# Row updates of five layer norms and the sums of a rotation, moved from GpSimd to VectorE in pieces

## The chip, the core and the metric

The kernel runs on one core of a Trainium2 chip. A core has a matrix engine (TensorE, PE in the profile), a vector engine (VectorE, DVE), a scalar engine (ScalarE, ACT), a general engine (GpSimd, POOL) and a queue engine that issues transfers (SyncE, SP). Each engine takes its instructions in order and waits for others on semaphores. The metric is the time of one execution on the device, in microseconds (us); of several runs the median is taken.

## The reference: what is computed

256 tokens of width 1024 pass through a first block of two layers in fp32. Each layer is a mixer, a cross attention to a memory of 256 tokens and a gated feed-forward net, with a layer norm of the scaled residual behind each:

```
for layer in range(DEPTH):                       # 2 layers
    mix = even_mixer(x, ...) or odd_mixer(x, ...)
    x  = layer_norm(DEEPNORM_ALPHA * x + mix, ln_g[layer, 0], ln_b[layer, 0])
    xa = memory_cross_attention(x, mem, ...)
    x  = layer_norm(DEEPNORM_ALPHA * x + xa, ln_g[layer, 1], ln_b[layer, 1])
    ff = swiglu(x, ffn_w_gu[layer], ffn_w_down[layer])
    x  = layer_norm(DEEPNORM_ALPHA * x + ff, ln_g[layer, 2], ln_b[layer, 2])

def layer_norm(x, g, b):
    ...
    return ((xf - mu) * lax.rsqrt(var + LN_EPS)).astype(x.dtype) * g + b

def rope(t):                                     # the odd mixer's queries and keys
    ...
    return jnp.concatenate([t1 * cos - t2 * sin, t1 * sin + t2 * cos], axis=-1).astype(t.dtype)
```

The even mixer joins a gated linear recurrence (mLSTM) and a neighbourhood attention, whose queries are scaled by 1/8 before a bias is added to the scores. The odd mixer is a differential attention with rotated queries and keys. A second block of two layers follows (convolutions, attention, and 16 experts); the change does not touch it.

## The kernel before

**Dense products.** Weights come as units of 128x2048 (`ring`, 1 MB) on SP's queue. `split` (L199) cuts each half of a unit exactly into two parts, `wh` (a copy on ScalarE, L126) and `wl` (the rest, a subtraction on VectorE, L123); the activations are split likewise into `xh` and `xl`. Three products (wh·xh, wh·xl, wl·xh) give fp32. A unit of 512 columns over 1024 rows is two `ring` loads, so four splits, of 12 products of 128x512 each. `wh` and `wl` have two buffers each, so a split's `wh` waits until TensorE is through with the split before the last. Work at the side is woven in: units of the modulation of the second block (`ada`: products with `scT`, then `adae`, then sums `mods`), and stretches of work (`fill`) such as the memory's keys and values (`mem_kv`) or the context's projection.

**Layer norms.** `resid` makes z = ALPHA·x + mix with its statistics; `ln_finish` (L288) takes them together, normalises z (first half on VectorE, L117, second on ScalarE, L132), transposes it by TensorE into X (`to_T`: `tov` copies from psum, then `xh` on ScalarE and `xl` on VectorE, with gain and bias by column), runs a `fill`, and then makes the new x itself, token-major: x = z·g, x = x + b, four GpSimd instructions of 128x1024, with g and b as rows broadcast over partitions (`lnbc`, two loads per norm). The products that follow read X; x is next read by the residual of the following norm. Six norms stand in the block; the last one makes x otherwise, so five have these updates. They follow the even mixer, cross attention, feed-forward, odd mixer and cross attention; below they are the first to fifth norm.

**Rotation.** `rope` (L708) makes for each of two token blocks four products with cos and sin out of psum (into `rtmp` and `tk`, VectorE) and two sums (`tk<-tk,rtmp`, GpSimd). `odd_mixer` does so for the first four of six units (0 and 1 are queries, 2 and 3 keys); the results are transposed by TensorE and copied into `qk` and `cpad`.

**Neighbourhood attention.** The bias `nab` is multiplied by 8 and the mask added, both on GpSimd; the softmax scales scores plus bias by 0.125.

**Order.** The instructions of each engine stand in an order that a scheduler sets at build time by priorities and dependences: `fill`, the modulation and the main line are ranked by it, and a tile whose memory another tile held waits for the last use of that one. z and the attention's queries `qk` share one slot; the odd mixer's slots lie where the slots of the feed-forward, with its norm's `lnbc`, were.

Of the kernel before, what the change touches and what calls it, by code (L numbers as in the profile page):

```python
# [46 lines left out]
class Net:  # L47
    def __init__(self, tc, a, out):
        self.tc, self.nc, self.a, self.out = tc, tc.nc, a, out
        self.S, self.bank = "M", "acc"  # L50
        self.wide, self.turn = False, 0
        self.tags, self.side, self.bg, self.ticks, self.every = {}, None, None, 0, 2
        self.later = []
        self.conv, self.rate, self.due = iter(()), (0, 0), 0.0

# [1 line left out]
    def ps(self):  # L57
        """psum for attention and transposes; work that fills gaps keeps off the bank ring it would wait for"""
# [5 lines left out]
    def open(self, side, **tags):  # L64
        """a pool of slots, by tag; closed in the reverse order on each side"""
# [12 lines left out]
    def t(self, shape, name, dt=F32, kind=None):  # L78
        """a slot of the smallest class that holds the tile"""
# [6 lines left out]
    def big(self, shape, name, dt=F32):  # L86
        """a slot that outlives the phase, where there are such"""
# [34 lines left out]
    def tt(self, out, in0, in1, op, eng=None):  # L122
        (eng or self.nc.vector).tensor_tensor(out=out, in0=in0, in1=in1, op=op)  # L123
# [16 lines left out]
    def rsqrt(self, v, n, g=None):  # L140
        """Newton's steps from the exponent's half; the steps' scales multiply to one"""
# [22 lines left out]
    def fill(self, n, bank="acc"):  # L164
        """n steps of the work at the side"""
# [10 lines left out]
    def after(self, f):  # L176
        """a part that waits for others: with the next step, where the work fills gaps"""
# [5 lines left out]
    def tick(self, n=1):  # L183
        """a modulation unit after every other unit of weights"""
# [15 lines left out]
    def split(self, src, eng=None, to=None):  # L200
        h, l = to or (self.tags[k][0].tile([128, 1024], F32R, name=k, bufs=self.tags[k][1]) for k in ("wh", "wl"))
        self.cp(h, src)
        self.tt(l, src, h.bitcast(F32), OP.subtract, eng=eng)
# [9 lines left out]
    def dense_unit(self, X, w, u, n=512, accs=None, nk=8):  # L213
        """[256, nk*128] @ [nk*128, n]; units of 2048 columns per partition."""
# [19 lines left out]
    def hl(self, X, c0, n, src, scale=1.0):  # L234
        """exact split of src (chunks c0..c0+n) into X's two parts"""
# [7 lines left out]
    def to_T(self, X, src, nch, g=None, b=None, c0=0, val=None):  # L243
        """src(t, c) token-major [128, 128] blocks -> chunks c0.. of X (or of val), times g plus b"""
# [17 lines left out]
    def acc_to_T(self, acc, t, dst, n=4, scale=1.0):  # L262
        """token-major psum [128, n*128] -> dst [128, n, 128]"""
# [24 lines left out]
    def ln_finish(self, z, st, x, i, fill, last=False):  # L288
# [25 lines left out]
        self.fill(fill)  # L314
        for t in range(2):
            self.tt(x[:, t], z[:, t], gb[0], OP.mult, eng=self.nc.gpsimd)
            self.tt(x[:, t], x[:, t], gb[1], OP.add, eng=self.nc.gpsimd)
# [11 lines left out]
    def softmax_T(self, scores, nh, nk, scale, bias=None, sinks=None):  # L329
        """scores(j, t, psum) fills [128 queries, nk*128] for head j of nh, block t of queries;  # L330
        -> the heads' [128 keys, nk, 256 queries] and their psum banks, free again.
        Two heads lie on different partitions, so that their products run side by side."""
# [60 lines left out]
    def even_mixer(self):  # L393
# [21 lines left out]
        # gates: rows i fwd, i bwd, f fwd, f bwd of 4 heads  # L415
# [7 lines left out]
        # log sigmoid of the forget gates  # L423
# [10 lines left out]
        for u, dst in ((2, bqT), (3, bkT)):  # L434
            accs = self.dense_unit(X, w, u)
            for t in range(2):
                self.acc_to_T(accs[t], t, dst[:, :, t * 128:(t + 1) * 128])
# [14 lines left out]
        # conv over tokens and silu; chunks 0..3 queries, 4..7 keys  # L452
# [25 lines left out]
    def mlstm(self, qk, vx, G, lf):  # L478
# [16 lines left out]
        # scores, transposed: [key, query] within a chunk  # L495
# [10 lines left out]
        for step in range(2):  # L506
            for d in range(2):
                t = step if d == 0 else 1 - step
                # transposed layout [s, l]: forward keeps s <= l
# [9 lines left out]
                if step == 0:  # L519
# [7 lines left out]
                    # state after this chunk  # L527
# [56 lines left out]
                for h in range(4):  # L584
                    o = hs[:, t, h * 128:(h + 1) * 128]
                    # block t: forward comes first for t == 0, backward for t == 1
# [7 lines left out]
    def neighbourhood(self, bqT, bkT, bv, Y):  # L594
        nc = self.nc
        rows = [slice(0, 64), slice(64, 128)]
        for hp in range(4):
            bias = []
            for hh in range(2):
# [3 lines left out]
                nc.gpsimd.tensor_scalar(b2, b2, 8.0, 0.0, op0=OP.mult, op1=OP.add)  # L603
# [6 lines left out]
            pts, P = self.softmax_T(scores, 2, 2, 0.125, bias=lambda j: bias[j])  # L610
# [1006 lines left out]
```

## Time and profile before

| | |
|---|---|
| three runs | 2421.43, 2418.28, 2417.38 us; median 2418.28 |
| profiled execution, span | 2420.6 us |
| TensorE busy | 2097.0 us (87%) |
| VectorE busy | 1186.0 us (49%) |
| ScalarE busy | 710.9 us (29%) |
| GpSimd busy | 105.0 us (4%), 64 instructions |

The profile gives, for one execution, each engine's busy time, groups of instructions by line and operation, time lines, and for idle time before an instruction what released it. [...]

### The profile page before, as it was taken

How to read it: one execution, taken by the hardware profiler on the slowest of the kernel's cores; microseconds unless marked ns; L12 is line 12 of the kernel's file. 1: busy time of each engine (PE TensorE's matmuls, PEld its weight loads, DVE VectorE, ACT ScalarE, POOL GpSimd, SP SyncE). 2: the span in 40 equal slices, each digit the busy share in tenths (PEclk: the TensorE clock that was granted, in tenths of full speed). 3: DMA queues.
4: the chain of work that ended last, by engine and by line, in shares of the span. 5: the costliest groups of instructions: out<-in, count | busy, mean ns of one | idle time of the engine just before them, and what ended most of it. 6: DMA issues, size and time to landing. Idle time of an engine off the chain costs nothing.

```text
span 2420.6 us, 26953 instructions
## 1 busy us (share of the span) xinstructions
PE 2097.0 (87%) x10408; PEld 1247.9 (52%) x10408; DVE 1186.0 (49%) x2530; ACT 710.9 (29%) x1183; POOL 105.0 (4%) x64
## 2 busy tenths in 40 slices
PE   8998999998998999999888999988887977666665
PEld 6775777776767777777665333322265621010100
DVE  6577575557678678567973122211179621010001
ACT  5444444443455434444442000000043510000000
POOL 0013010003101100000000000000000000000000
PEclk9999999999999999999987999999988977776767
DMA  8644466665534354446427999999963289999997
GB/s 292 243 183 174 157 224 245 243 244 194 186 127 154 131 170 169 157 139 226 158 96 304 421 421 421 421 421 421 421 237 113 74 361 421 422 421 421 421 422 308
DMA packets 93296, 652.68 MB, mean 270 GB/s; under 512 B 10480, under 2 KB 10992, under 8 KB 15472
## 3 DMA queue, kind: packets, MB, share of 16 engines
q1 hardware_dynamic: 93168, 650.96, 69.3%
q8 instruction: 82, 1.34, 0.2%
q14 instruction: 46, 0.38, 0.0%
HBM read 649.87 MB, written 1.05 MB: 269 GB/s over the span
## 4 chain that ended last, share of the span: by engine, by line
PE 35%; DMA 29%; DVE 10%; ACT 2%; issue 1%; POOL 1%; DVEq 0%; SPq 0%; POOLq 0%; ACTq 0%
PE acc L107 22%; DMA ring<-in_w_up_dram 18%; DMA ring<-in_w_dn_dram 11%; PE ps L107 10%; PE ps L110 3%; DVE wl L123 2%; DVE cvo L120 1%; ACT wh L126 1%; DVE xl L123 1%; POOL tk L123 1%; PE acc L110 0%; DVE tk L123 0%; DVE z L120 0%; ACT sx_e L132 0%; DVE my L123 0%
## 5 line engine op out<-in xcount | busy, mean ns | idle before, releaser
L123 DVE TENSOR_TENSOR wl<-ring,wh 128x1024 fp32r<-128x1024 f32 x346 | 432.4, 1252 | 258.0 <-ACT wh L126 251.7
L126 ACT ACTIVATE wh<-ring 128x1024 fp32r<-128x1024 f32 x346 | 366.0, 1059 | 453.3 <-PE acc L107 312.6
L107 PE MATMUL acc<-ring,XS 128*64 128x512 f32 (+1 forms) x2048 | 411.7, 702 | 92.9 <-DMA ring<-in_w_up_dram 48.2
L107 PE MATMUL acc<-wl,xh 128*128 128x512 f32 (+1 forms) x736 | 291.8, 401 | 16.3 <-DVE wl L123 15.9
L107 PEld LDWEIGHTS acc<-ring,XS 128*64 128x64 f32 (+1 forms) x2048 | 96.3, 130 | 395.8 <-issue 150.7
L107 PE MATMUL acc<-wh,xh 128*128 128x512 f32 (+1 forms) x736 | 292.1, 400 | 8.9 <-ACT xh L126 5.6
L107 PE MATMUL acc<-wh,xl 128*128 128x512 f32 (+1 forms) x736 | 292.4, 397 | 5.9 <-DVE xl L123 5.9
L107 PE MATMUL acc<-ring,hTm 128*64 128x512 f32 (+1 forms) x1024 | 206.3, 695 | 51.6 <-DMA ring<-in_w_dn_dram 50.9
L120 DVE SCALAR_TENSOR_TENSOR mth<-mth,acc 128x512 f32<-128x512 f32 x24 | 16.5, 688 | 467.0 <-ACT mth L132 467.0
L132 ACT ACTIVATE mth<-acc 128x512 f32<-128x512 f32 x24 | 14.3, 597 | 733.2 <-PE acc L107 733.2
L107 PEld LDWEIGHTS acc<-wl,xh 128*128 128x128 f32 x736 | 142.3, 195 | 53.7 <-DVE wl L123 23.9
L107 PEld LDWEIGHTS acc<-wh,xh 128*128 128x128 f32 x736 | 143.0, 195 | 41.7 <-ACT xh L126 7.3
L107 PEld LDWEIGHTS acc<-wh,xl 128*128 128x128 f32 x736 | 143.3, 195 | 38.7 <-DVE xl L123 9.6
L107 PEld LDWEIGHTS acc<-ring,hTm 128*64 128x64 f32 (+1 forms) x1024 | 47.4, 130 | 196.2 <-DMA ring<-in_w_dn_dram 108.7
L107 PE MATMUL ps<-wh,xh 128*128 128x512 f32 x368 | 146.1, 397 | 2.5 <-ACT wh L126 2.5
L107 PE MATMUL ps<-wl,xh 128*128 128x512 f32 x368 | 145.4, 397 | 2.8 <-DVE wl L123 2.7
L107 PE MATMUL ps<-wh,xl 128*128 128x512 f32 x368 | 146.0, 397 | 0.0
L123 DVE TENSOR_TENSOR my<-acc,gy 128x512 f32<-128x512 f32 x24 | 16.6, 692 | 233.4 <-PE acc L107 233.4
L107 PE MATMUL ps<-my,GT 128*128 128x512 f32 x160 | 85.8, 680 | 19.4 <-DVE my L123 19.4
L120 DVE SCALAR_TENSOR_TENSOR cvo<-pb,cols,cvo 128x256 f32<-128x256 f32 x180 | 81.8, 477 | 0.3
L107 PEld LDWEIGHTS ps<-wh,xh 128*128 128x128 f32 x368 | 69.6, 189 | 20.4 <-ACT wh L126 4.5
L107 PEld LDWEIGHTS ps<-wl,xh 128*128 128x128 f32 x368 | 69.2, 189 | 20.3 <-DVE wl L123 4.1
(473 smaller groups left out, 2642.7 us busy)
## 6 DMA issues: line engine op xcount, KB each, us to landing
ring<-in_w_gate_dram SPq DMA_DIRECT2D x128, 1024.0 KB, 19.8
ring<-in_w_up_dram SPq DMA_DIRECT2D x128, 1024.0 KB, 19.8
ring<-in_w_dn_dram SPq DMA_DIRECT2D x128, 1024.0 KB, 19.8
ring<-in_w_ada_dram SPq DMA_DIRECT2D x48, 1024.0 KB, 4.9
ring<-in_w_gu_dram SPq DMA_DIRECT2D x44, 1024.0 KB, 4.8
ring<-in_w_in_dram SPq DMA_DIRECT2D x29, 1024.0 KB, 4.9
ring<-in_w_down_dram SPq DMA_DIRECT2D x22, 1024.0 KB, 4.9
ring<-in_w_memkv_dram SPq DMA_DIRECT2D x16, 1024.0 KB, 4.9
```

What stands on the lines that cost most here:

```text
L107: self.nc.tensor.matmul(out, lhsT=lhsT, rhs=rhs, start=start, stop=stop)
L110: self.nc.tensor.transpose(out, in_, self.ident)
L120: (eng or self.nc.vector).scalar_tensor_tensor(out, in0, s, in1, op0=op0, op1=op1)
L123: (eng or self.nc.vector).tensor_tensor(out=out, in0=in0, in1=in1, op=op)
L126: self.nc.scalar.activation(out=out, in_=in_, func=AF.Copy, scale=scale)
L132: self.nc.scalar.activation(out=out, in_=in_, func=func, **kw)
```

## The change

- `tt` returns its instruction, and a list `lazy` is kept. After the subtraction of each weight split of the main line (VectorE, not in a fill), `split` takes one entry off the list and issues it right after that subtraction.
- `ln_finish` no longer issues four GpSimd instructions of 128x1024, but puts two empty entries and eight pieces of 128x512 on the list, for VectorE. So the ten splits behind a norm carry them: the first two none, the next eight one piece each.
- `rope`'s two sums go to VectorE.
- In the neighbourhood attention the queries are scaled by 0.125 in the copy out of psum, the multiplication of the bias by 8 goes, and the softmax's scale is 1. The addition of the mask stays on GpSimd.

(Lines shift by one to ten: L123 becomes L124.)

```diff
@@ split
-        self.tt(l, src, h.bitcast(F32), OP.subtract, eng=eng)
+        last = self.tt(l, src, h.bitcast(F32), OP.subtract, eng=eng)
+        if self.lazy and eng is None and self.S == "M":
+            f = self.lazy.pop(0)
+            if f is not None:
+                with self.tc.issue_after(last.ins):
+                    f()
@@ ln_finish
-        for t in range(2):
-            self.tt(x[:, t], z[:, t], gb[0], OP.mult, eng=self.nc.gpsimd)
-            self.tt(x[:, t], x[:, t], gb[1], OP.add, eng=self.nc.gpsimd)
+        self.lazy += [None] * 2
+        for t in range(2):
+            for u in range(2):
+                c = slice(u * 512, (u + 1) * 512)
+                for j, (src, op) in enumerate(((z, OP.mult), (x, OP.add))):
+                    self.lazy.append(lambda t=t, c=c, j=j, src=src, op=op:
+                                     self.tt(x[:, t, c], src[:, t, c], gb[j][:, c], op))
@@ even_mixer
-        for u, dst in ((2, bqT), (3, bkT)):
+        for u, dst, scale in ((2, bqT, 0.125), (3, bkT, 1.0)):
...
-                self.acc_to_T(accs[t], t, dst[:, :, t * 128:(t + 1) * 128])
+                self.acc_to_T(accs[t], t, dst[:, :, t * 128:(t + 1) * 128], scale=scale)
...
-                nc.gpsimd.tensor_scalar(b2, b2, 8.0, 0.0, op0=OP.mult, op1=OP.add)
...
-            pts, P = self.softmax_T(scores, 2, 2, 0.125, bias=lambda j: bias[j])
+            pts, P = self.softmax_T(scores, 2, 2, 1.0, bias=lambda j: bias[j])
@@ rope
-        self.tt(dst[:, :, 0], dst[:, :, 0], tmp[:, :, 0], OP.subtract, eng=self.nc.gpsimd)
-        self.tt(dst[:, :, 1], dst[:, :, 1], tmp[:, :, 1], OP.add, eng=self.nc.gpsimd)
+        self.tt(dst[:, :, 0], dst[:, :, 0], tmp[:, :, 0], OP.subtract)
+        self.tt(dst[:, :, 1], dst[:, :, 1], tmp[:, :, 1], OP.add)
```

VectorE in the odd mixer, at the rotation of unit 0, before (`acc_4603` and `acc_4604` are that unit's two token blocks; the sums stand on GpSimd; a split's number here is its place in the odd mixer):

```order
L123 TENSOR_TENSOR wl_4675<-ring_4656,wh_4674 128x1024
L123 TENSOR_TENSOR wl_4723<-ring_4720,wh_4722 128x1024
L123 TENSOR_TENSOR rtmp_4691<-acc_4603,tabs_67 128x8x32 x2
L123 TENSOR_TENSOR tk_4690<-acc_4603,tabs_67 128x8x32 x2
L123 TENSOR_TENSOR rtmp_4705<-acc_4604,tabs_67 128x8x32 x2
L123 TENSOR_TENSOR tk_4704<-acc_4604,tabs_67 128x8x32 x2
L123 TENSOR_TENSOR wl_4739<-ring_4720,wh_4738 128x1024
```

The same place now (`acc_4599` and `acc_4600` are unit 0, `wl_4840` and `wl_4857` the ninth and tenth split, which belong to unit 2):

```order
L124 TENSOR_TENSOR wl_4791<-ring_4771,wh_4790 128x1024
L124 TENSOR_TENSOR x_71<-x_71,lnbc_4412 128x512
L124 TENSOR_TENSOR wl_4840<-ring_4837,wh_4839 128x1024
L124 TENSOR_TENSOR x_71<-z_4400,lnbc_4410 128x512
L124 TENSOR_TENSOR wl_4857<-ring_4837,wh_4856 128x1024
L124 TENSOR_TENSOR x_71<-x_71,lnbc_4412 128x512
L124 TENSOR_TENSOR rtmp_4689<-acc_4599,tabs_67 128x8x32 x2
L124 TENSOR_TENSOR tk_4688<-acc_4599,tabs_67 128x8x32 x2
L124 TENSOR_TENSOR tk_4688<-tk_4688,rtmp_4689 128x8x32 x2
L124 TENSOR_TENSOR rtmp_4703<-acc_4600,tabs_67 128x8x32 x2
L124 TENSOR_TENSOR tk_4702<-acc_4600,tabs_67 128x8x32 x2
L124 TENSOR_TENSOR tk_4702<-tk_4702,rtmp_4703 128x8x32 x2
```

Each wl now carries a piece, and the rotation of unit 0, which stood between the first two splits of unit 1 (the fifth and sixth), stands behind the tenth split and its piece; the rotation of unit 1 follows it.

TensorE at the same place now, the end of unit 1 (`acc_4717`), a modulation unit, the transposes of unit 0 and the start of unit 2 (`acc_4835`):

```order
L108 MATMUL acc_4717<-wh_4790,xh_4447 128x512
L108 MATMUL acc_4717<-wh_4790,xl_4448 128x512
L108 MATMUL acc_4717<-wl_4791,xh_4447 128x512
L108 MATMUL acc_4756<-ring_4754,scT_97 32x256 x8
L111 MATMUL ps_4696<-tabs_67,tk_4688 128x128 x3
L111 MATMUL acc_4756<-tabs_67,adae_4765 128x128 x2
L111 MATMUL ps_4696<-tabs_67,tk_4688 128x128
L111 MATMUL ps_4710<-tabs_67,tk_4702 128x128 x4
L108 MATMUL acc_4835<-wh_4839,xh_4447 128x512
```

Before, these transposes stood within the first split of unit 1; now TensorE meets them after all of unit 1 and ahead of unit 2.

VectorE in the cross attention after the fourth norm, now (`wl_6546` and `wl_6562` are the last splits of the context's projection, `wl_6598` the first of the output weights, `ps_6270` to `ps_6368` the transposed queries):

```order
L124 TENSOR_TENSOR wl_6546<-ring_6543,wh_6545 128x1024
L124 TENSOR_TENSOR wl_6562<-ring_6543,wh_6561 128x1024
L124 TENSOR_TENSOR wl_6598<-ring_6595,wh_6597 128x1024
L124 TENSOR_TENSOR x_71<-z_5769,lnbc_5919 128x512
L124 TENSOR_TENSOR cva_6577<-cva_6577,acc_6507 128x256
L130 COPY qk_6195<-ps_6270 128x4x128
L130 COPY qk_6195<-ps_6278 128x4x128
L130 COPY qk_6195<-ps_6360 128x4x128
L130 COPY qk_6195<-ps_6368 128x4x128
```

Before, the first two of these copies stood ahead of the last splits of the query weights and the other two behind the first split of the context's projection; now all four stand behind its last split and the last piece that reads z.

## Rows read from the trace of the kernel before

**Rows 1.** The page: busy time, share and instructions by engine; the costliest group.

```profile
PE 2097.0 (87%) x10408; PEld 1247.9 (52%) x10408; DVE 1186.0 (49%) x2530; ACT 710.9 (29%) x1183; POOL 105.0 (4%) x64
...
L123 DVE TENSOR_TENSOR wl<-ring,wh 128x1024 fp32r<-128x1024 f32 x346 | 432.4, 1252 | 258.0 <-ACT wh L126 251.7
```

**Rows 2.** GpSimd's groups, whole span: busy us, mean ns, idle before, releaser.

```profile
L123 POOL TENSOR_TENSOR x<-x,lnbc 128x1024 f32<-128x1024 f32 x10 | 29.6, 2977 | 0.0
L123 POOL TENSOR_TENSOR x<-z,lnbc 128x1024 f32<-128x1024 f32 x10 | 27.4, 2759 | 525.2 <-issue 223.7 <-ACT z L132 214.0 <-DVE z L117 86.8
L123 POOL TENSOR_TENSOR tk<-tk,rtmp 128x256 f32<-128x256 f32 x16 | 15.1, 974 | 45.2 <-DVE tk L123 45.2
...
L603 POOL TENSOR_SCALAR nab<-nab 128x512 f32<-128x512 f32 x8 | 6.0, 747 | 185.7 <-DMA nab<-in_rpb_dram 185.3
```

**Rows 3.** VectorE's time line, without GpSimd: start, length, instruction, [idle before, releaser].

```profile
731.52 0.69 DVE L123 TENSOR_TENSOR xl<-tov,xh 128x512 fp32r<-128x512 f32 x1
...
736.44 0.81 DVE L117 TENSOR_SCALAR z<-z,rq_zM,lnmM 128x1024 f32<-128x1024 f32 x1
...
575.30 1.23 DVE L123 TENSOR_TENSOR wl<-ring,wh 128x1024 fp32r<-128x1024 f32 x1 [1.54 <-ACT wh L126]
```

**Rows 4.** Time line at the first norm, VectorE and TensorE.

```profile
227.20 2.97 DVE L117 TENSOR_SCALAR z<-z,rq_zM,lnmM 128x1024 f32<-128x1024 f32 x1
...
233.49 6.89 DVE L123 TENSOR_TENSOR xl<-tov,xh 128x512 fp32r<-128x512 f32 x4 [0.30 <-ACT xh L126]
...
230.23 1.97 PE L110 MATMUL ps<-tabs,z 128*128 128x128 f32 x16 [1.48 <-DVE z L117]
...
241.57 0.50 PE L107 MATMUL acc<-wl,xh 128*128 128x512 f32 x1 [3.46 <-DVE wl L123]
242.01 1.94 PE L107 MATMUL acc<-ring,scT 128*32 128x256 f32 x16
```

**Rows 5.** Windows: length, busy (instructions) of PE, PEld, DVE, ACT, POOL; PEclk, DMA, GB/s.

```profile
241.50:245.30 3.80, 3.73 (x20) 1.84 (x21) 1.15 (x2) 0.38 (x1) 0.00 (x0) 0.56 0.44 119
563.00:566.20 3.20, 3.18 (x8) 2.53 (x9) 3.20 (x2) 0.00 (x0) 2.19 (x1) 0.50 0.44 182
570.00:578.00 8.00, 8.00 (x37) 6.43 (x35) 4.38 (x11) 3.19 (x3) 0.34 (x1) 1.00 0.69 251
```

**Rows 6.** Time line at the second norm: VectorE, ScalarE, TensorE.

```profile
318.91 2.33 DVE L123 TENSOR_TENSOR mods<-mods,cols 128x4 f32<-128x4 f32 x1
...
322.86 1.02 ACT L132 ACTIVATE tov<-ps,cols 128x256 f32<-128x256 f32 x2 [3.45 <-DVE tov L117]
...
327.87 0.50 PE L107 MATMUL ps<-wh,xh 128*128 128x512 f32 x1 [2.50 <-ACT wh L126]
...
328.76 1.07 PE L107 MATMUL ps<-ring,scT 128*32 128x256 f32 x16
...
332.52 0.50 PE L107 MATMUL ps<-wl,xh 128*128 128x512 f32 x1 [2.69 <-DVE wl L123]
```

**Rows 7.** Time line at the third norm: VectorE and TensorE.

```profile
557.20 3.02 DVE L123 TENSOR_TENSOR wl<-ring,wh 128x1024 fp32r<-128x1024 f32 x1
560.14 6.81 DVE L123 TENSOR_TENSOR xl<-tov,xh 128x512 fp32r<-128x512 f32 x4
...
563.02 0.80 PE L107 MATMUL acc<-wh,xl 128*128 128x512 f32 x1 [4.73 <-DVE xl L123]
```

**Rows 8.** Time line of TensorE at the fourth and the fifth norm.

```profile
746.90 0.63 PE L107 MATMUL acc<-wl,xh 128*128 128x512 f32 x1 [2.79 <-DVE wl L123]
...
850.54 0.58 PE L107 MATMUL acc<-wl,xh 128*128 128x256 f32 x1 [3.02 <-DVE wl L123]
```

**Rows 9.** Time line in the odd mixer, units 0 and 1: VectorE, GpSimd, TensorE.

```profile
576.50 0.76 DVE L123 TENSOR_TENSOR rtmp<-acc,tabs 128x256 f32<-128x256 f32 x2
...
577.66 3.77 POOL L123 TENSOR_TENSOR tk<-tk,rtmp 128x256 f32<-128x256 f32 x4 [12.47 <-DVE tk L123]
...
581.49 0.66 PE L110 MATMUL ps<-tabs,tk 128*128 128x128 f32 x4 [1.11 <-POOL tk L123]
```

More of the change, by code (lines that the diff above doesn't have):

```diff
@@ L54, in __init__ @@
         self.conv, self.rate, self.due = iter(()), (0, 0), 0.0
+        self.lazy = []
     def ps(self):
@@ L122, in tt @@
     def tt(self, out, in0, in1, op, eng=None):
-        (eng or self.nc.vector).tensor_tensor(out=out, in0=in0, in1=in1, op=op)
+        return (eng or self.nc.vector).tensor_tensor(out=out, in0=in0, in1=in1, op=op)
     def cp(self, out, in_, scale=1.0):
```

## The prediction

> **What bounds the kernel now.** I read the page first [rows 1]. TensorE is busy for 2097.0 us, 87% of the span, GpSimd for 105.0 us, 4%. The reader should see from this that GpSimd's work counts only where TensorE waits for it, or for something that it slows. So the second step is GpSimd's instructions by group [rows 2], and the third the time line around each place where they run, with TensorE's idle time and its releaser in brackets. The second block, from about 920 us, holds no instruction of the change; I take time saved ahead of it to arrive in full at the end.
>
> What the time lines show is one pattern, five times. After a layer norm, GpSimd runs four row updates (x<-z and x<-x, 27.4 + 29.6 us for all five norms [rows 2]). In just that time those instructions of VectorE are long that work on SBUF alone. An xl of 128x512 takes 0.69 us alone [rows 3]; beside GpSimd four of them take 6.89 us [rows 4] instead of 4 x 0.69 = 2.8. A z of 128x1024 takes 0.81 us alone [rows 3] and 2.97 beside GpSimd [rows 4]. TensorE needs exactly these.
>
> **Row updates leave GpSimd: what comes back.** I go norm by norm, and take as gain the idle time of TensorE that the lengthened instructions explain.
> - First norm [rows 4]: 1.48 us before the transposes of z, and 3.46 us before the product that needs wl: 4.9 us. Both go, since z is done 2.2 us and xl 4.1 us earlier. After the second gap the granted clock is 0.56 [rows 5]; the 16 products with scT take 1.94 us there, against 1.07 at the second norm [rows 6], and some four behind them are slow as well (0.2 each). That is 1.6 us. Together 6.5.
> - Second norm [rows 6]: 2.69 us before wl goes whole. The other gap, 2.50 us, is released by ScalarE's wh, but that stands on ScalarE behind tov copies, which wait 3.45 us for VectorE's tov, and this stands behind a mods of 128x4 that takes 2.33 us. I count 2.0 of it. Together 4.7.
> - Third norm [rows 7]: 4.73 us before xl. Without the long wl (3.02 us, against 1.23 alone [rows 3]: 1.8 less) and with xl at 0.69, the second xl is done near 559.7 instead of 563 us, so 3.4 us come back. [...] Eight times 0.18 is another 1.5. Together 4.9.
> - Fourth and fifth norm [rows 8]: 2.79 and 3.02 us before wl, and the same slow products behind each gap, 1.5: 4.3 and 4.5. Gaps before GpSimd starts, or that ScalarE's own queue explains, are not counted.
> The sum is 6.5 + 4.7 + 4.9 + 4.3 + 4.5 = 24.9 us. The lower bound, without the clock and without the gap that ScalarE released, is 4.9 + 2.7 + 3.4 + 2.8 + 3.0 = 16.8. I take the upper value, because TensorE's clock is at its full level in the stretch without gaps [rows 5].
>
> **The 40 pieces on VectorE.** Each is 128x512 from SBUF like xl: 0.69 us [rows 3], 40 x 0.69 = 27.6 us of VectorE's time. A piece stands behind the wl of one weight split and ahead of the next, so the next wl, and through it TensorE, is queued behind it. In a dense stretch VectorE idles 1.54 us before a wl, waiting for ScalarE's wh [rows 3], so that a piece fits with 0.85 us to spare and costs nothing. That cover is thin where a split has other VectorE work as well (copies of kd and KT, sums of the modulation). I allow 1.5 us, five late wl of 0.3; the bounds are 0 and, if no piece were hidden, 27.6. The loads of the row vectors lnbc now stand a few weight loads later in SP's queue; they are used long after they land, and I take 0.
>
> [...]
>
> **What the pieces hold back.** The order shows two places where later work now stands behind the last pieces.
> - Odd mixer. The rotation of units 0 and 1 comes behind the wl and the piece of the tenth split, and that split's wh needs one of two buffers, which TensorE frees only at the end of the eighth, which is the end T of unit 1. From T: wh about 1.1, wl 1.23, the piece 0.69, four multiplications of the first token block 1.5 (two take 0.76 [rows 9]) and two sums of 0.4. The first transposes start near T+5.2; the second block is ready 2.3 later, unit 1 in the same manner, between copies, at about T+14.5. TensorE has 10.7 us of work up to the end of the tenth split and gets there at T+16.2: 5.5 us idle. Before, each of these two units had a gap of 1.11 [rows 9], so this is 3.3 net. A long gap is followed by a low clock at the third norm, so 1.5 more. I take 4.8; the bounds are 1 (if the rotation's first half suffices to keep TensorE going) and 7.
> - Cross attention after the fourth norm. The copies into qk stand behind the last x<-z, which waits for the first split of the output weights, and this stands behind all four splits of the context's projection. TensorE ends that projection and then waits for a piece, a sum of 0.4 and two copies of about 0.6: 2.0 us. The bounds are 0 and 4. In the first cross attention the same tie costs nothing, since no projection stands between.
>
> **Rotation sums.** GpSimd's 16 sums took 0.97 us each [rows 2], four of them 3.77 us, and TensorE waited 1.11 us for the last ones in each of four units [rows 9]. On VectorE a sum of 128x256 is about 0.4 us (estimated from two multiplications of the same size in 0.76). In units 2 and 3 the last sum is then ready some 0.8 us earlier: 2 x 0.85 = 1.7 us gained, bounds 0 and 2.3. Units 0 and 1 are in the item above.
>
> **Neighbourhood attention.** The scale moves into a copy that ScalarE makes anyway, and 8 GpSimd instructions of 0.75 us go [rows 2]. They run on GpSimd ahead of need; no idle time of TensorE names them. I take 0, bounds 0 and 1 gained.
>
> **Sum.** 24.9 + 1.7 - 1.5 - 4.8 - 2.0 = 18.3 us off. The profiled span, 2420.6 us, is 2.3 above the median of 2418.28 and inside the three runs (2417.38 to 2421.43), so I take the difference off the median: 2418.3 - 18.3 = 2400.
>
> **Rivals.**
> - The next limit stands close behind (0.17). ScalarE's chain of tov, xh and wh after each norm is not shortened. If TensorE runs into it, half of the 24.9 comes back: 12.4 + 1.7 - 1.5 - 6.8 = 5.8 off, 2412.5. For it: one gap names ScalarE's wh already [rows 6]. Against it: the longest gap of each norm names VectorE [rows 4, 6 to 8].
> - More comes back (0.07). The two places that are held back cost their lower bounds, 1 and 0, and the pieces nothing: 24.9 + 2.3 - 1 = 26.2 off, 2392.
> - Slower: VectorE becomes the bound (0.07). In the ten splits after each norm a piece makes the next wl late. This decides where the idle time before wl is under 0.69 us; over all 346 splits its mean is 258.0/346 = 0.75 [rows 1], far less than 1.54. Then all 27.6 us lie on the path: 2418.3 - 24.9 - 1.7 + 27.6 + 6.8 = 2426.1. Against it: once TensorE has caught up after a norm, its 12 products of 0.22 us set the pace, 2.7 us to a split, and VectorE needs 1.23 + 0.69 of that.
> - It does not do what it says (0.03): VectorE is long at those places for another reason than GpSimd. Then the 24.9 fall away and the costs stay: 2418.3 - 1.7 + 1.5 + 6.8 = 2424.9. Against it: the same xl takes 0.69 us at 731.52, shortly before GpSimd's updates of the fourth norm [rows 3].
>
> **How the numbers follow.** The forecast has 0.66. A measurement of this kernel tells about 0.2%, 4.8 us, from no change, so faster means below 2413.4. The forecast and the better case, 0.73, lie there, and half of the close limit: 0.81. Its other half, with a little of the slower cases, is within 0.2%: 0.10. Slower keeps 0.09. The range leaves out the slower rivals and the far ends of the others: from 2389 (both places cheap, and some more of the gap at the second norm back) to 2415 (the close limit, with one of them dear).
>
> **What would show it.** Right: no idle time of TensorE released by wl or xl at the five norms, four xl in 2.8 us, and one new gap in the odd mixer with the rotation on VectorE as its releaser. Wrong: no idle time before wl in the splits with pieces while TensorE waits for wl (VectorE bound); gaps after the norms that name wh or xh (close limit); wl and xl as long as before with GpSimd idle (another reason).

## The result, and the profile after

The changed kernel takes 2390.70 us (median of four runs, 2383.67 to 2392.36); the kernel before, beside it, 2418.46 (2417.38 to 2421.43). The ratio is 0.9878, 95% interval 0.9861 to 0.9895: faster by 1.2%, 25 to 34 us. The forecast was 2400, 18.3 us off, with a range of 2389 to 2415. Its direction held, its size did not: the ratio puts the time at 2388.8 on the median of before, just below the range, and the gain is one and a half times what the sum gave.

The page of the changed kernel, the lines that answer to [rows 1], and GpSimd's costliest group over the whole span (busy us, mean ns, idle before), which answers to [rows 2]:

```profile
PE 2077.5 (87%) x10408; PEld 1241.2 (52%) x10408; DVE 1180.9 (49%) x2586; ACT 711.0 (30%) x1183; POOL 26.6 (1%) x20
...
L124 DVE TENSOR_TENSOR wl<-ring,wh 128x1024 fp32r<-128x1024 f32 x346 | 422.6, 1223 | 245.2 <-ACT wh L127 239.5
```

```profile
L124 POOL TENSOR_TENSOR nab<-nab,tabs 128x512 f32<-128x512 f32 x8 | 11.1, 1409 | 188.9 <-PE acc L108 151.1 <-DMA nab<-in_rpb_dram 37.7
```

GpSimd went from 105.0 to 26.6 us. VectorE took over 40 pieces and 16 sums and is nevertheless busy for 5 us less than before: what it waited beside GpSimd counted as busy time, and a wl now takes 1223 ns on the mean instead of 1252.

**Where the time came from.** The same instruction at each norm (lnmM, on VectorE) is a good mark; the first transposes of tk stand ahead of the first norm and the first KT,QT product behind the feed-forward. Time lines of the kernel before, and then of the changed one (start, length, instruction):

```profile
128.78 0.44 PE L110 MATMUL acc<-tabs,tk 128*128 128x128 f32 x2 [0.97 <-ACT tk L126]
...
225.30 0.15 DVE L120 SCALAR_TENSOR_TENSOR lnmM<-lnmv,rq_zM 128x2 f32<-128x2 f32 x1
...
316.96 0.16 DVE L120 SCALAR_TENSOR_TENSOR lnmM<-lnmv,rq_zM 128x2 f32<-128x2 f32 x1
...
552.30 0.15 DVE L120 SCALAR_TENSOR_TENSOR lnmM<-lnmv,rq_zM 128x2 f32<-128x2 f32 x1
...
735.77 0.15 DVE L120 SCALAR_TENSOR_TENSOR lnmM<-lnmv,rq_zM 128x2 f32<-128x2 f32 x1
...
834.72 0.15 DVE L120 SCALAR_TENSOR_TENSOR lnmM<-lnmv,rq_zM 128x2 f32<-128x2 f32 x1
...
932.89 0.70 PE L107 MATMUL ps<-KT,QT 64*128 64x256 f32 x4 [0.62 <-DVE QT L129]
```

```profile
129.61 0.44 PE L111 MATMUL acc<-tabs,tk 128*128 128x128 f32 x2 [0.97 <-ACT tk L127]
...
223.11 0.16 DVE L121 SCALAR_TENSOR_TENSOR lnmM<-lnmv,rq_zM 128x2 f32<-128x2 f32 x1
...
308.33 0.16 DVE L121 SCALAR_TENSOR_TENSOR lnmM<-lnmv,rq_zM 128x2 f32<-128x2 f32 x1
...
538.95 0.15 DVE L121 SCALAR_TENSOR_TENSOR lnmM<-lnmv,rq_zM 128x2 f32<-128x2 f32 x1
...
719.34 0.15 DVE L121 SCALAR_TENSOR_TENSOR lnmM<-lnmv,rq_zM 128x2 f32<-128x2 f32 x1
...
813.70 0.15 DVE L121 SCALAR_TENSOR_TENSOR lnmM<-lnmv,rq_zM 128x2 f32<-128x2 f32 x1
...
904.61 0.70 PE L108 MATMUL ps<-KT,QT 64*128 64x256 f32 x4 [0.61 <-DVE QT L130]
```

The differences of neighbouring marks give the stages. A second profile of each kernel (two runs further down) has the same marks, and the table sets both beside the forecast, whose terms are put where they belong:

| stage | before, us (first, second profile) | after, us | measured | forecast |
|---|---|---|---|---|
| tk to first norm (neighbourhood attention) | 96.5, 96.3 | 93.5, 93.7 | -3.0, -2.7 | 0 |
| first to second norm | 91.7, 91.3 | 85.2, 85.2 | -6.4, -6.0 | -6.5 |
| second to third norm | 235.3, 235.3 | 230.6, 230.8 | -4.7, -4.5 | -4.7 |
| third to fourth norm (third norm, odd mixer) | 183.5, 183.6 | 180.4, 181.9 | -3.1, -1.7 | -4.9 - 1.7 + 4.8 = -1.8 |
| fourth to fifth norm (with cross attention) | 99.0, 99.0 | 94.4, 94.4 | -4.6, -4.5 | -4.3 + 2.0 = -2.3 |
| fifth norm to KT,QT | 98.2, 98.2 | 90.9, 91.0 | -7.3, -7.2 | -4.5 |
| pieces, anywhere | | | none seen | +1.5 |
| sum | | | -29.1, -26.6 | -18.3 |

The second block, from KT,QT to the end, took 1487.7 us in the first profile of before and 1484.7 in that of the changed kernel; over all profiles of this study it lies between 1478 and 1488, with no tie to the kernel. The gain arises ahead of 930 us and reaches the end.

**First norm after**, to be read beside [rows 4]. VectorE's and TensorE's time lines:

```profile
224.69 0.81 DVE L118 TENSOR_SCALAR z<-z,rq_zM,lnmM 128x1024 f32<-128x1024 f32 x1
...
229.87 1.29 DVE L124 TENSOR_TENSOR xl<-tov,xh 128x512 fp32r<-128x512 f32 x2 [0.30 <-ACT xh L127]
231.82 1.29 DVE L124 TENSOR_TENSOR xl<-tov,xh 128x512 fp32r<-128x512 f32 x2 [0.66 <-ACT xh L127]
...
233.30 0.50 PE L108 MATMUL acc<-wh,xh 128*128 128x512 f32 x1 [0.50 <-ACT wh L127]
...
234.99 1.07 PE L108 MATMUL acc<-ring,scT 128*32 128x256 f32 x16
```

z takes 0.81 us instead of 2.97, four xl 2.6 instead of 6.89; xl now waits for ScalarE's xh. The gaps of 1.48 and 3.46 us are gone, and the 16 products with scT take 1.07 us again. ScalarE's wh is next in line, as the first rival had it, but with 0.50 us only.

**Odd mixer after.** VectorE around the last piece, then TensorE's gap:

```profile
569.77 1.22 DVE L124 TENSOR_TENSOR wl<-ring,wh 128x1024 fp32r<-128x1024 f32 x1 [0.89 <-ACT wh L127]
570.91 0.68 DVE L124 TENSOR_TENSOR x<-x,lnbc 128x512 f32<-128x512 f32 x1
571.51 0.74 DVE L124 TENSOR_TENSOR rtmp<-acc,tabs 128x256 f32<-128x256 f32 x2
...
573.02 1.93 PE L108 MATMUL acc<-ring,scT 128*32 128x256 f32 x16 [4.15 <-issue]
```

Between the piece of the split before and this wl VectorE still idles 0.89 us, the 0.85 of the forecast: the piece is hidden. The forecast's new gap is here too, 4.15 us before the modulation's products. The view names no releaser; the order and the times say that these products need the bank that the rotation frees: the last product out of that bank (tk<-acc) is done at 572.92, the gap ends at 573.02. The 16 products behind it take 1.93 us, against 1.07 at the first norm: the granted clock (PEclk in the views, the share of its full clock that TensorE was granted) is 0.50 from 572 to 578 us.

### The profile page after: what moved, and what is told of

Same layout as the page of the kernel before. It is cut to its first block, busy times and chain, and to the rows that moved or that the text cites. A ratio compares the mean times of both kernels' runs of the same rounds, so it can differ in the third digit from the quotient of the medians.

```text
span 2389.3 us, 26933 instructions
## 1 busy us (share of the span) xinstructions
PE 2077.5 (87%) x10408; PEld 1241.2 (52%) x10408; DVE 1180.9 (49%) x2586; ACT 711.0 (30%) x1183; POOL 26.6 (1%) x20
## 4 chain that ended last, share of the span: by engine, by line
PE 53%; DMA 33%; DVE 10%; ACT 3%; issue 1%; SPq 0%; POOL 0%; DVEq 0%; ACTq 0%; POOLq 0%
PE acc L108 32%; DMA ring<-in_w_up_dram 20%; PE ps L108 17%; DMA ring<-in_w_dn_dram 12%; PE ps L111 3%; DVE wl L124 3%; ACT wh L127 1%; DVE cvo L121 1%; PE acc L111 1%; ACT xh L127 0%; DVE z L121 0%; ACT sx_e L133 0%; DMA ring<-in_w_even_dram 0%; DVE tk L124 0%; DVE rq_tM L118 0%
## 5 line engine op out<-in xcount | busy, mean ns | idle before, releaser
L124 DVE TENSOR_TENSOR wl<-ring,wh 128x1024 fp32r<-128x1024 f32 x346 | 422.6, 1223 | 245.2 <-ACT wh L127 239.5
L124 DVE TENSOR_TENSOR my<-acc,gy 128x512 f32<-128x512 f32 x24 | 16.6, 692 | 233.7 <-PE acc L108 233.7
L108 PE MATMUL ps<-my,GT 128*128 128x512 f32 x160 | 80.5, 644 | 19.4 <-DVE my L124 19.4
L108 PEld LDWEIGHTS ps<-wh,xl 128*128 128x128 f32 x368 | 69.2, 188 | 16.8 <-issue 3.5
```

Of the source, the lines that this page charges most:

```text
L108: self.nc.tensor.matmul(out, lhsT=lhsT, rhs=rhs, start=start, stop=stop)
L124: return (eng or self.nc.vector).tensor_tensor(out=out, in0=in0, in1=in1, op=op)
```

## The experiments

All ratios are to runs of the kernel before on the same chip. First each part alone.

**Neighbourhood attention alone**, on the kernel before:

```diff
-        for u, dst in ((2, bqT), (3, bkT)):
+        for u, dst, scale in ((2, bqT, 0.125), (3, bkT, 1.0)):
...
-                nc.gpsimd.tensor_scalar(b2, b2, 8.0, 0.0, op0=OP.mult, op1=OP.add)
...
-            pts, P = self.softmax_T(scores, 2, 2, 0.125, bias=lambda j: bias[j])
+            pts, P = self.softmax_T(scores, 2, 2, 1.0, bias=lambda j: bias[j])
```

> The kernel before with the change in the neighbourhood attention alone (scale in the queries' copy, no multiplication of the bias by 8). Theory: the 2.2 us by which the first norm came earlier in the changed kernel come from this edit, since nothing else of the change stands ahead of that norm; the first norm's lnmM stands near 223 us instead of 225.3 and the time is 2.2 to 3 us lower, about 2415.8. Rival, as in the prediction: the edit is worth 0 to 1 us, the earlier norm is a difference between executions; the first norm stays near 225.3 and the time at 2418.

Measured: 2416.24 against 2420.05, ratio 0.9993 (0.9981 to 1.0006), which includes no change and includes 3 us. The stage from tk to the first norm is 93.5 us (131.06 to 224.56), the 93.5 and 93.7 of the changed kernel, against 96.5 and 96.3. Over all thirteen profiles of the study that stage is 96.3 to 99.2 us in the four without the edit and 92.5 to 95.8 in the nine with it. A stretch of low clock can stand just ahead of the norm: with short instructions on GpSimd (further down) the granted clock is 0.50 from 222 to 228 us, and the norm's mark stands at 226.39. A mark ahead of such stretches is finer: the xl of the attention's last pair of heads stands 84.2 to 85.1 us behind the first transposes of tk without the edit, and 80.9 to 82.2 with it. VectorE in the kernel before, at a sum of scores and bias and at that xl, and then that xl with the edit alone:

```profile
204.41 0.69 DVE L123 TENSOR_TENSOR sx_s<-ps,nab 128x512 f32<-128x512 f32 x1 [0.56 <-POOL nab L123]
...
213.50 0.42 DVE L123 TENSOR_TENSOR xl<-ps,xh 128x256 fp32r<-128x256 f32 x1 [1.99 <-ACT xh L126]
```

```profile
212.95 0.42 DVE L123 TENSOR_TENSOR xl<-ps,xh 128x256 fp32r<-128x256 f32 x1 [1.30 <-ACT xh L126]
```

Counted from 128.78 and 131.06 these are 84.7 and 81.9 us. So some 3 us belong to this edit; the whole time is not fine enough to show it alone.

**Rotation sums alone**, on the kernel before:

```diff
-        self.tt(dst[:, :, 0], dst[:, :, 0], tmp[:, :, 0], OP.subtract, eng=self.nc.gpsimd)
-        self.tt(dst[:, :, 1], dst[:, :, 1], tmp[:, :, 1], OP.add, eng=self.nc.gpsimd)
+        self.tt(dst[:, :, 0], dst[:, :, 0], tmp[:, :, 0], OP.subtract)
+        self.tt(dst[:, :, 1], dst[:, :, 1], tmp[:, :, 1], OP.add)
```

> The kernel before with only the rotation's 16 sums on VectorE; the row updates stay on GpSimd. Theory: each of the four gaps of 1.11 to 1.19 us before the transposes shrinks to about 0.3, so 3.4 us less, 2415. Rival: VectorE's sums make the next wl late instead, the gap before the transposes is replaced by one before wl, and the time stays at 2418.

Measured: 2416.20, ratio 0.9987 (0.9975 to 0.9998), 3 us less. None of the four gaps before the transposes is left, and none takes their place: from 575 to 650 us TensorE waits for no instruction that the profile names. The full 4.6 us of idle time went, 1.15 per unit and not 0.85.

**Row updates alone**, in pieces on VectorE, the other two edits undone:

> The kernel before with only the row updates of the five norms as pieces on VectorE; sums and neighbourhood attention as before. Theory: the parts add, so this gives what is left of 27.8 us without 2.2 (neighbourhood) and about 1.7 (rotation): 24 off, 2394.5, and the stages first to second norm, second to third and fifth norm to the end of the feed-forward are 6.5, 4.6 and 7 us shorter than before, as in the changed kernel. Rival: part of the gain needs the other edits (sums that left GpSimd free, another order), and this is worth under 20 us, above 2398.

Measured: 2395.55, ratio 0.9908 (0.9892 to 0.9924), 22 us less. First to second norm takes 86.5 us, second to third 230.9, fifth norm to KT,QT 92.5: within 1.6 us of the changed kernel. With 1.7 and 3.1 us of the two runs above the parts add up to 27, against 29.5 for all (from the ratios): as far as intervals of 3 to 4 us to either side tell, they add.

Next, what it is about the row updates: the engine, the moment, or the length of one instruction.

**Whole rows on VectorE at the old place**, on the changed kernel:

```diff
-        self.lazy += [None] * 2
...
+        for t in range(2):
+            self.tt(x[:, t], z[:, t], gb[0], OP.mult)
+            self.tt(x[:, t], x[:, t], gb[1], OP.add)
```

> The changed kernel, but the row updates run on VectorE as whole rows of 128x1024 where GpSimd had them, four at a time behind the norm, not in pieces between splits. Theory: what cost time was that VectorE was held up just after the norm, and 4 x 1.23 = 4.9 us of own work there holds it up about as long as GpSimd did (4.1 us on xl, 1.8 on wl): the gaps before xl or wl come back at some 2 to 3 us each, about 2403. Rival: only the engine matters, and VectorE has room wherever the updates stand: 2391.

Measured: 2411.79, ratio 0.9964 (0.9951 to 0.9977): most of the gain is gone, more than expected. TensorE's time line at the second norm and behind the fourth:

```profile
327.47 0.50 PE L108 MATMUL ps<-wh,xh 128*128 128x512 f32 x1 [2.15 <-ACT wh L127]
330.79 1.22 PE L108 MATMUL acc<-wl,fh 128*128 128x512 f32 x2 [2.12 <-DVE wl L124]
...
744.90 1.22 PE L108 MATMUL acc<-wl,xh 128*128 128x512 f32 x2 [7.17 <-DVE wl L124]
```

GpSimd is idle there, and yet the gaps are back: 4.9 us of VectorE's own work just behind the norm hold TensorE up as GpSimd's did. Of the 9 us that are left, some 5 are the other two edits, which this run keeps (1.7 and 3.1 alone), so another engine alone is worth about 4 of the 22 us; the spreading makes the rest.

**The old instructions on GpSimd, but later**, on the changed kernel; a small GpSimd instruction that reads the third split's wl goes ahead of them:

```diff
+        self.part = l
...
+        def late():
+            self.nc.gpsimd.tensor_scalar(x[:, :, 0], self.part.bitcast(F32)[:, 0:2], 1.0, 0.0, op0=OP.mult, op1=OP.add)
+            for t in range(2):
+                self.tt(x[:, t], z[:, t], gb[0], OP.mult, eng=self.nc.gpsimd)
+                self.tt(x[:, t], x[:, t], gb[1], OP.add, eng=self.nc.gpsimd)
+        self.lazy += [None] * 2 + [late]
```

> The changed kernel, but the row updates stay on GpSimd as four instructions of 128x1024 and start only after the third weight split behind the norm (a small GpSimd instruction ahead of them reads that split's wl). Theory: the moment decides, not the engine: in the dense stretch VectorE has 1.5 us of idle time per split, wl may be long there (up to 3 us) and TensorE waits little; 2391 to 2395. Rival: what GpSimd takes from VectorE costs the same wherever it runs, about 4 to 6 us per norm: 2410 to 2418.

Measured: 2407.98, ratio 0.9952 (0.9935 to 0.9970), between the two (this run and the next keep the other two edits as well). At the first two norms the theory holds. VectorE behind the second norm, while GpSimd runs from 326.88 on:

```profile
328.21 2.42 DVE L124 TENSOR_TENSOR wl<-ring,wh 128x1024 fp32r<-128x1024 f32 x1 [1.50 <-ACT wh L127]
330.99 2.98 DVE L124 TENSOR_TENSOR wl<-ring,wh 128x1024 fp32r<-128x1024 f32 x1 [0.35 <-ACT wh L127]
```

wl takes twice its time, VectorE's idle time absorbs it, and TensorE has no gap named wl; the stages behind the first and the second norm take 86.7 and 232.7 us instead of 91.7 and 235.3. Behind the third norm TensorE waits 2.65 us for a wl, and behind the fourth the theory fails: 7.37 us for a wl, and this is VectorE before it, with GpSimd's instructions of that time in the second fence:

```profile
741.64 2.38 DVE L116 TENSOR_SCALAR rq_nF<-hn_s2F 128x4 f32<-128x4 f32 x1
743.94 0.16 DVE L118 TENSOR_SCALAR rq_yF<-rq_aF 128x4 int32<-128x4 int32 x1
744.13 2.23 DVE L124 TENSOR_TENSOR rq_tF<-rq_yF 128x4 f32<-128x4 f32 x1
746.39 2.26 DVE L124 TENSOR_TENSOR rq_tF<-rq_tF,rq_nF 128x4 f32<-128x4 f32 x1
748.69 2.26 DVE L121 SCALAR_TENSOR_TENSOR rq_zF<-rq_tF,rq_yF 128x4 f32<-128x4 f32 x1
```

```profile
741.57 2.43 POOL L124 TENSOR_TENSOR x<-z,lnbc 128x1024 f32<-128x1024 f32 x1
743.96 2.38 POOL L124 TENSOR_TENSOR x<-z,lnbc 128x1024 f32<-128x1024 f32 x1
746.29 2.34 POOL L124 TENSOR_TENSOR x<-x,lnbc 128x1024 f32<-128x1024 f32 x1
748.59 2.34 POOL L124 TENSOR_TENSOR x<-x,lnbc 128x1024 f32<-128x1024 f32 x1
```

Instructions on 128x4 numbers, 0.16 us alone, take 2.2 to 2.4 us: each ends when a GpSimd instruction ends, one after the other through all four. That is 2.1 to 2.2 us lost by each, as by an xl of 128x512 (0.69 to 2.90 us): the price is by the instruction, not by the byte. The expectation's rival (equal cost anywhere) is wrong as well; what counts is how many such VectorE instructions fall beside GpSimd, and whether TensorE waits for them.

**Short instructions on GpSimd at the old place** put that to the test, each row update cut into 128x256:

```diff
-        self.lazy += [None] * 2
...
+        for j, op in ((0, OP.mult), (1, OP.add)):
+            for t in range(2):
+                for q in range(4):
+                    c = slice(q * 256, (q + 1) * 256)
+                    self.tt(x[:, t, c], (x if j else z)[:, t, c], gb[j][:, c], op, eng=self.nc.gpsimd)
```

> The changed kernel, but the row updates run on GpSimd at their old place, right behind the norm, each of the four instructions of 128x1024 cut into four of 128x256. Theory: GpSimd holds what VectorE's instructions with two SBUF inputs need for one whole GpSimd instruction, and lets one of them in between two of its own (xl 0.69, 2.90, 2.86, 0.69 us beside instructions of 2.8 us); with instructions of about 0.6 us an xl or wl loses 0.6 us instead of 2.2, the gaps at the norms shrink to a quarter, and without the hold in the odd mixer the time is 2385 to 2395. Rival: both engines share a bandwidth, so that the same bytes on GpSimd cost VectorE the same: gaps as before the change, 2410 to 2416.

Measured: 2396.19, ratio 0.9901 (0.9887 to 0.9916), just above the range of the theory and far from the rival's. First norm, VectorE, then TensorE at the first, second and fifth norm, then GpSimd's groups:

```profile
234.59 4.58 DVE L124 TENSOR_TENSOR xl<-tov,xh 128x512 fp32r<-128x512 f32 x4 [0.30 <-ACT xh L127]
```

```profile
240.88 0.50 PE L108 MATMUL acc<-wl,xh 128*128 128x512 f32 x1 [1.66 <-DVE wl L124]
...
326.95 0.50 PE L108 MATMUL ps<-wl,xh 128*128 128x512 f32 x1 [0.96 <-DVE wl L124]
...
836.66 1.22 PE L108 MATMUL ps<-wl,xh 128*128 128x512 f32 x2 [3.20 <-DVE wl L124]
```

```profile
L124 POOL TENSOR_TENSOR x<-x,lnbc 128x256 f32<-128x256 f32 x40 | 43.5, 1121 | 0.0
L124 POOL TENSOR_TENSOR x<-z,lnbc 128x256 f32<-128x256 f32 x40 | 42.4, 1097 | 547.4 <-ACT z L133 469.6 <-DVE z L118 77.8
```

GpSimd now does the same work in 85.9 us instead of 57.0, and costs TensorE less: gaps of 3.46 and 2.69 fall to 1.66 and 0.96, to a half and a third and not to a quarter, since these instructions take 1.1 us and not the 0.6 of the theory. At the fifth norm nothing is gained (3.20); the cause stays open.

Then the terms that were off, and the gap in the odd mixer.

**Fifth norm alone back on GpSimd**, on the changed kernel (`if i == 4:` the four old instructions):

> The changed kernel with the row updates of the fifth norm alone back on GpSimd, where they were. Theory: the fifth norm's stage was mis-sized in the prediction because GpSimd there costs an idle gap of 3.0 us and two stretches of low clock (4 and 7 us long, about 4 us lost): the time goes up by 7 us to 2398, with a granted clock near 0.59 in both stretches. Rival, as in the prediction: 4.5 us, 2395, with one low stretch.

Measured: 2393.01, ratio 0.9891 (0.9869 to 0.9912). Against the changed kernel's 0.9878 the whole time does not tell 2 us from 7. The stage does: 97.5 us (814.98 to 912.49) against 90.9, 6.6 more. TensorE's gap, then the window behind it (columns as in [rows 5]):

```profile
830.78 0.58 PE L108 MATMUL acc<-wl,xh 128*128 128x256 f32 x1 [4.56 <-DVE wl L124]
```

```profile
828.00:836.00 8.00, 5.22 (x19) 4.68 (x20) 6.38 (x14) 0.00 (x0) 0.00 (x0) 0.57 0.55 193
```

There is one low stretch, not two: 8 us at 0.57, which loses 8 x 0.43 = 3.4 us. The idle gap is longer (4.56) than before the change (3.02). From the end of the gap before cvb to the end of this one it is 8.60 us here (822.18 to 830.78) and 8.56 before (841.98 to 850.54): VectorE's wl sets that time, and the slow products that stood there before the change (842 to 846, granted 0.59) only filled the wait. The theory's sum holds, its split does not.

**Two pieces per split behind the third norm**, so that the rotation need not wait:

```diff
-        self.lazy += [None] * 2
+        self.lazy += [None] * 2 if i != 2 else []
...
+                self.lazy += [lambda fs=fs: [f() for f in fs]] if i == 2 else fs
```

> The changed kernel, but behind the third norm two pieces follow each of the first four splits (no empty entries), so that the rotation of unit 0 has not to wait for the tenth split. Theory: the gap of 4.15 us near 573 us and the low clock behind it go, 4 to 6 us less, 2386. Rival: two pieces (1.3 us) do not fit behind a wl right after the norm, wl comes late in unit 0, and the gain is under 2 us.

Measured: 2385.64, ratio 0.9854 (0.9829 to 0.9878). The gap of 4.15 us is gone and from 566 to 600 us TensorE has no named gap at all; third to fourth norm takes 176.3 us instead of 180.4. Two pieces fit behind a wl.

**The same, and the four multiplications of each norm ahead of its additions:**

> As the run with two pieces per split behind the third norm, and at every norm the four multiplications come ahead of the four additions, so that z is free four splits after the norm's first piece instead of seven and the queries' copies in the two cross attentions do not wait for the output weights' first split. Theory: the gap of 1.09 us before the scores after the fourth norm goes as well: about 1 us less than that run, 2385. Rival: the copies were not what those scores waited for, no difference.

Measured: 2384.49, ratio 0.9854 (0.9830 to 0.9877): no difference that can be told from the run above, although the gap before the scores is gone. It is the fastest median of the study, 36 us below the kernel before on its chip. Third to fourth norm is 171.8 us here, 4.5 less than in the run above, with the same idle gaps to 0.3 us: the granted clock makes it. By length x (1 - granted clock) it lost 6.8 us there in the run above (674 to 696) and 1.7 here (708 to 714).

**Both kernels once more**, for a second profile:

> The kernel before, once more, for a second profile. Theory: the stretches of low clock behind TensorE's gaps differ from one execution to the next by some us (in the first profile 12 us were lost to them ahead of 930 us, at the first, third, fourth and fifth norm and once in the odd mixer), while the idle gaps are the same to 0.2 us. Rival: the low stretches stand at the same places and are as long, so that each belongs to its gap.

> The changed kernel, once more, for a second profile. Theory: the idle gaps (4.15 us near 573, 1.09 us before the scores after the fourth norm, 2.02 before cvb) are the same to 0.2 us; the stretches of low clock (6.8 us lost in the first profile, near 570 and 690) vary. Rival: they are the same as well.

Measured: 2418.01 and 2385.99. Idle gaps are the same nearly everywhere (before: 3.44, 2.70, 4.72, 2.80, 3.02 us; after: 4.16, 1.09, 2.02); one gap of before moved (1.48 before the transposes of z became 1.88 before a product with wh). Low clock, by the same measure in slices ahead of 930 us (where TensorE idles within a slice, that part costs nothing): before it lost 12.0 and 13.7 us, at the same five places, with the one at the first norm twice as long in the second; after it lost 6.8 and 8.5, with one place more (678 to 686) and one half as long (572 to 578). So neither side is right alone: the places mostly recur, their number and length change by 1.7 to 3.4 us. Windows of the first profiles, at the fifth norm before, and then of the changed kernel:

```profile
842.00:846.00 4.00, 3.95 (x19) 3.71 (x20) 4.00 (x2) 1.36 (x2) 4.00 (x2) 0.59 0.27 104
850.00:858.00 8.00, 7.46 (x29) 6.55 (x30) 4.14 (x9) 0.68 (x1) 0.00 (x0) 0.60 0.38 131
```

```profile
570.00:578.00 8.00, 4.98 (x29) 3.54 (x30) 7.83 (x21) 0.38 (x1) 0.00 (x0) 0.57 0.65 204
690.00:698.00 8.00, 6.70 (x21) 5.10 (x20) 3.12 (x5) 2.29 (x3) 0.00 (x0) 0.57 0.78 297
```

## Why the prediction was right and wrong

- **What bounds, and the pattern.** Right. GpSimd's updates slowed VectorE, and TensorE waited for VectorE; the row updates alone are 22 us, and the lengthened instructions at the first norm are back at their own time (z 0.81, four xl 2.6 us).
- **Row updates, norm by norm.** First and second norm came out as summed, 6.4 and 4.7 against 6.5 and 4.7, and these were the two whose stage holds nothing else. The fifth was mis-sized: 4.5 forecast, 7.3 measured. I took the slow products behind the gap from the third norm, 1.5 us, as "the same", without a window of their own. The eight times 0.18 of the third norm are read from [rows 5]: 8 products take 3.18 us there at a granted clock of 0.50, 0.40 each, and 37 take 8.00 us at 1.00, 0.22 each. At the fifth norm, between 850 and 858, the clock lost 8 x 0.40 = 3.2 us. And the gap of 3.02 us was itself shortened by slow products ahead of it (842 to 846, 4 x 0.41 = 1.6 us): with the fifth norm back on GpSimd, where the one low stretch lies behind the gap, it is 4.56.
- **Pieces.** Their own duration and cover were right (0.68 us, 0.89 to spare). The allowance of 1.5 us found no late wl.
- **Odd mixer.** The place and the kind were right: 4.15 us at one gap, against 5.5 forecast. Unit 1 ended at T = 573.02 - 4.15 = 568.87; wl was done at 570.99, T+2.1, and the rotation began at T+2.6 where I had T+3.0, since one VectorE instruction starts a little before the one ahead of it has ended (the piece at 570.91 with wl done at 570.99, rtmp at 571.51 with the piece done at 571.59: 0.08 us each). TensorE waited there not for the sums and the transposes, as I had it, but already for the modulation's products ahead of them. The other gaps that I summed for this place were too small to be named. The low clock behind the gap was more than I charged (3.4 and 1.7 us in the two profiles, a part of it within the gap itself, against 1.5).
- **Cross attention after the fourth norm.** The wait is there, before the product with qk, with 1.09 us and not 2.0. Gap (2.79) and clock (1.7) of the fourth norm were 4.5, so the rest of the stage, some 1.2 us, lies in gaps too small to name.
- **Rotation.** 1.15 us per unit came back, not 0.85: VectorE's sums leave no gap (four units alone: 4.6 us of idle time).
- **Neighbourhood attention. The step that failed.** I took 0, with bounds 0 and 1, because these instructions "run on GpSimd ahead of need" and no idle time of TensorE names them. The stage is 2.7 to 3.0 us shorter. They did not run ahead of need: over that stage VectorE's sums of scores and bias wait 4.2 us for nab in the kernel before, among it 0.67, 0.41 and 0.56 us before the second sum of each of the last three pairs of heads, and with the edit no second sum waits. Counted from the first transposes of tk, the xl of the four pairs come 0, 0.9, 3.0 and 2.8 us earlier with the edit alone. That TensorE's idle time did not name them was no reason for 0 either: by releaser it is 9.2 and 7.9 us in the two profiles of before, 7.3 with the edit alone and 8.1 in the changed kernel, so the named waits do not carry the 3 us. The order changed too (in sum VectorE waits for nab no less with the edit, 6.0 us), and how the earlier sums reach TensorE stays open.
- **The sum.** Of the 10.8 us that were missing by the first profiles (8.3 by the second), 3.0 are the neighbourhood attention, 2.8 the fifth norm, 2.3 the fourth norm with its attention, 1.5 the allowance for the pieces, and 1.3 the stage of the third norm and the odd mixer; in the second profiles that last stage came as summed (-1.7 against -1.8), and between the two the clock decides. Nearly all errors had one sign: gains were taken lower than they came, and the costs of the pieces and of the cross attention higher.
- **Rivals.** The close limit did not decide: what is left at the first three norms is 0.50 and 0.72 us before a product with ScalarE's wh, and 0.78 us before one with VectorE's xl. The time came nearest the second rival (2392), but by luck and not by its way: the pieces cost nothing, as it had it, while the two places cost 4.15 and 1.09 us and not 1 and 0, and what it lacked lay in the neighbourhood attention and the fifth norm. VectorE as the bound did not appear with pieces, but VectorE's own work did hold TensorE up with whole rows at the old place (2411.8): the spreading is what avoids it.

## What to carry to other kernels

A light engine off the critical path can cost a good part of its busy time (22 of 57.0 us for the row updates), if its long instructions hold off the engine that feeds TensorE: count the VectorE instructions that fall beside it, not the bytes (2.1 to 2.2 us were lost by 128x4 and by 128x512 alike). Moving such work is worth most when it also goes away from the critical moment, in pieces shorter than the idle time that the view of waits shows before the next needed instruction (0.68 us in 1.5). And whatever waits for the last piece, by a shared slot as much as by data, moves with it: two pieces per split behind the third norm took a gap of 4.15 us away, and the pieces that free a shared slot put first took one of 1.09. An instruction that no idle time of TensorE names is not free by that: ask whether an engine that feeds TensorE waits for it, as VectorE did for nab.

## What the runs showed of the hardware

GpSimd's row updates and VectorE's xl took turns by whole instructions. The first three of the four xl of the first norm before, which [rows 4] shows as one group of 6.89 us, one by one, and the GpSimd instructions beside them:

```profile
233.49 0.69 DVE L123 TENSOR_TENSOR xl<-tov,xh 128x512 fp32r<-128x512 f32 x1 [0.30 <-ACT xh L126]
234.10 2.90 DVE L123 TENSOR_TENSOR xl<-tov,xh 128x512 fp32r<-128x512 f32 x1
236.92 2.86 DVE L123 TENSOR_TENSOR xl<-tov,xh 128x512 fp32r<-128x512 f32 x1
```

```profile
233.59 2.86 POOL L123 TENSOR_TENSOR x<-x,lnbc 128x1024 f32<-128x1024 f32 x1
236.41 2.82 POOL L123 TENSOR_TENSOR x<-x,lnbc 128x1024 f32<-128x1024 f32 x1
```

The second xl starts while GpSimd's instruction runs (233.59 to 236.45) and ends 0.55 us after it, as if it had begun then; the third does the same with the next one (to 239.23), and the fourth meets none. The first goes ahead of GpSimd's: it ends at 234.18 in its own 0.69 us, and GpSimd's instruction ends 2.27 us after that, so of its 2.86 us it seems to have waited 0.5 as well (others of its size take 2.34). The time lost is 2.1 to 2.2 us by 128x512 (0.69 to 2.90 and 2.86) and by 128x4 (0.15 to 2.33 at the second norm [rows 6]) alike, and the turns alternate, one VectorE instruction to one of GpSimd. Two inputs in SBUF, which the theory of the short instructions named, were not needed: z reads one tensor and two columns and took 2.97 us instead of 0.81 [rows 3, 4], and rq_nF, out of hn_s2F alone, took 2.38 in the run with GpSimd later. VectorE's tov out of psum were not lengthened: the 20 of 128x256 took 0.53 to 0.55 us each in both kernels, among them four at the first norm before (231.30 to 233.19) beside a GpSimd instruction (230.25 to 233.63).

TensorE's granted clock fell to 0.50 behind the gaps of 2.79 to 4.73 us at the first, third, fourth and fifth norm (0.56 from 241.5 to 245.3, 0.50 from 563 to 566.2, 0.50 from 747.2 to 750.4 and 0.60 from 850 to 858 in the first profile of the kernel before), and not behind those of 2.50 and 2.69 us at the second (1.00 from 300 to 350), in either profile of that kernel. It fell also near the odd mixer's end, behind gaps of 1.89 and 1.30 us close together (690 to 698 in the changed kernel, granted 0.57), and in that kernel's second profile behind 1.51 and 0.69 us too (678 to 686, granted 0.57). The gap before cvb (1.99 us before the change, 2.02 after) was followed by a low clock before (842 to 846, granted 0.59) and by the full one after (820 to 828, granted 1.00). From one execution to the next such a stretch came twice as long (at the first norm before: 0.50 from 240 to 246 in the second profile), or not at all (678 to 686 in the changed kernel: 1.00 in the first profile). With the same idle gaps, what was lost to the low clock ahead of 930 us differed by 1.7 us between the two profiles of each kernel (12.0 and 13.7, 6.8 and 8.5); a forecast of a few us should carry that.
